# Two small tiles of a one-layer encoder kernel grow by 32 bytes

## The chip, the core and the metric

The kernel runs on one core of a Trainium2 chip. The core has TensorE for matmuls (its weight loads are shown as PEld), VectorE (DVE), ScalarE (ACT), GpSimd (POOL) and SyncE (SP), which issues most DMAs. The metric is the device time of one execution in microseconds. SBUF, the working memory, has 128 partitions; a tile takes the same address range in each of them, and "address" below means the byte offset within a partition.

## What is computed

One layer of a streaming encoder on 256 tokens of width 2048, in float32. RMS norm of x feeds one large projection; three mixers work on its columns (chunked attention, a diagonal state-space scan, an mLSTM matrix memory), are gated, merged and projected; then follow cross attention over 256 memory tokens and a SwiGLU block, each with a residual.

```python
h = _rms(x, norm_mix[i])
qa, ka, va, us, xm, vm, om, im, fm, gpre = jnp.split(h @ w_in[i], splits, axis=-1)
ya = _chunk_attention(qa, ka, va, ...)
ys = _s5(us, ...)
ym = _mlstm(xm, vm, om, im, fm, ...)
merged = (gates[:, :, 0] * (ya @ w_br_a[i]) + gates[:, :, 1] * (ys @ w_br_s[i])
          + gates[:, :, 2] * (ym @ w_br_m[i]))
x = x + merged @ w_out[i]
x = x + _mem_attention(_rms(x, norm_x[i]), mem_n, w_xq[i], w_xkv[i], g_xq[i], g_xk[i], w_xo[i])
x = x + _swiglu(_rms(x, norm_ffn[i]), w_gu[i], w_down[i])
```

## The kernel before

Every large product is done in three matmuls on the type float32r. Both operands are split into a high and a low part, and high x high, high x low and low x high are summed in PSUM. The weights come by DMA into `raw`, 2048 columns at a time; `split_w` (lines 110 to 118) makes `whi` on ScalarE (L116) and `wlo` on VectorE (L117). The activations are split once for each stage, by `split_act` (L206, L207, or L209, L210 with a gain), into the operand tiles `xT`, `mT`, `eT`, `x1T`, `oT`, `x2T`, `hT`, each with an `_h` and an `_l`.

Two helpers run the products. In `gemm_i` (L146, L147, L148) the activation tile is the loaded, stationary operand, 128 columns of it, and up to 512 columns of the split weights stream through. In `gemm_ii` (L169, L170, L171) the weights are loaded and 256 tokens of the activation stream. A matmul and the load of the next one's stationary operand overlap. Cross attention does its scores (L960) and its output (L986) in the same split type with 256 columns.

The stages run in this order: the input projection with the three mixers woven into it, the branch outputs, `w_out`, the memory's keys and values, the cross attention, `w_xo`, then gate and up projection (22 blocks) and the last projection `w_down`. The order on each engine is set when the program is built, by a scheduler that knows shapes and priorities.

Addresses come from pools. A pool gives each tag one or more buffers, and pools lie one behind the other in the order in which they are opened: `const`, `wp` (raw, whi, wlo), `scr` (small scratch tiles, among them `am`, 64 bytes in a partition, at L569), and behind `scr` all that the stages use: `poolA` (xT, later eT and oT), `p1`, `s5`, `p2`, `p3` (hT). Two pools are opened from the right end of the memory: `poolB` (L810; tags Bh and Bl for mT, x1T and x2T) and `px1` (the residual x1) to the left of it. A tile's size thus shifts all that is placed behind it. Sizes are rounded up to 32 bytes.

`am` holds 16 values for each partition, the mLSTM gate terms of 4 heads, 2 token tiles and 2 kinds. VectorE and ScalarE write it in `m_gates`; `m_core` reads columns of it as biases.

Of the kernel before, what the change touches and what calls it, by code (L numbers as in the profile page):

```python
# [9 lines left out]
F32 = mybir.dt.float32  # L10
F32R = mybir.dt.float32r
# [7 lines left out]
P = 128  # L19
T = 256  # L20
D = 2048
KD = D // P
# [30 lines left out]
def tile_block(ctx: ExitStack, tc: tile.TileContext, a: dict, out: bass.AP):  # L53
# [6 lines left out]
    scr = ctx.enter_context(tc.tile_pool(name="scr", bufs=4))  # L60
# [3 lines left out]
    def nm(s):  # L64
        uid[0] += 1
        return f"{s}_{uid[0]}"
# [5 lines left out]
    def sm():  # L72
        t = ps.tile([P, 512], F32, tag="sm", name=nm("sm"))
        return t
# [184 lines left out]
    def vexp(dst, src, n):  # L259
        def tt(s):  # L260
            return p1.tile([P, 32], F32, tag="ve_" + s, name=nm("ve_" + s), bufs=1)[:, :n]
        x, kf, r, pz = tt("x"), tt("k"), tt("r"), tt("p")
        V.tensor_scalar(x, src, -120.0, 120.0, ALU.max, ALU.min)
        V.tensor_scalar(kf, x, 1.4426950408889634, MAGIC, ALU.mult, ALU.add)
        V.tensor_scalar(kf, kf, MAGIC, None, ALU.subtract)
        V.scalar_tensor_tensor(r, kf, -0.693359375, x, ALU.mult, ALU.add)
        V.scalar_tensor_tensor(r, kf, 2.12194440e-4, r, ALU.mult, ALU.add)
        c = [1.0 / 5040, 1.0 / 720, 1.0 / 120, 1.0 / 24, 1.0 / 6, 0.5, 1.0]
        V.tensor_scalar(pz, r, c[0], None, ALU.mult)
        for ci in c[1:]:  # L270
            V.scalar_tensor_tensor(pz, pz, ci, r, ALU.add, ALU.mult)

        k1 = tt("k1")
        V.tensor_scalar(k1, kf, 0.5, MAGIC, ALU.mult, ALU.add)
        V.tensor_scalar(k1, k1, MAGIC, None, ALU.subtract)
        V.tensor_tensor(kf, kf, k1, ALU.subtract)
        V.tensor_scalar(pz, pz, 1.0, None, ALU.add)
        for kx in (k1, kf):
            ki = p1.tile([P, 32], I32, tag="ve_i", name=nm("ve_i"), bufs=2)[:, :n]
            V.tensor_scalar(kx, kx, 127.0, 8388608.0, ALU.add, ALU.mult)  # L280
            V.tensor_copy(ki, kx)
            V.tensor_tensor(pz, pz, ki.bitcast(F32), ALU.mult)
        V.tensor_copy(dst, pz)
# [247 lines left out]
    def m_gates():  # L531

        g = ymv["if"]
        zf = g[:, :, 4:8]

        def t8(s):
            return scr.tile([P, 2, 4], F32, tag="g8_" + s, name=nm("g8_" + s), bufs=1)
        fl = lambda x: x.rearrange("p t h -> p (t h)")
        az, e, y, y2, s_ = t8("az"), t8("e"), t8("y"), t8("y2"), t8("s")
        V.scalar_tensor_tensor(az, zf, -1.0, zf, ALU.mult, ALU.min)  # L540
        vexp(fl(e), fl(az), 8)
        V.tensor_scalar(y, e, 2.0, None, ALU.add)
        V.reciprocal(y, y)
        V.tensor_tensor(y, y, e, ALU.mult)
        V.tensor_tensor(y2, y, y, ALU.mult)
        V.tensor_scalar(s_, y2, 2.0 / 17, None, ALU.mult)
        for d in (15, 13, 11, 9, 7, 5, 3):
            V.scalar_tensor_tensor(s_, s_, 2.0 / d, y2, ALU.add, ALU.mult)
        V.scalar_tensor_tensor(s_, s_, 2.0, y, ALU.add, ALU.mult)
        V.tensor_scalar(az, zf, 0.0, None, ALU.min)  # L550
        V.tensor_tensor(az, az, s_, ALU.subtract)
        pt = sm()
        for t in range(2):
            PE.transpose(pt[0:4, t * P:(t + 1) * P], az[:, t], ident)
            PE.transpose(pt[0:4, T + t * P:T + (t + 1) * P], g[:, t, 0:4], ident)
        rows = p1.tile([4, 5, T], F32, tag="V", name="rows")
        V.tensor_copy(rows[:, 0:2], pt[0:4, :].rearrange("p (k t) -> p k t", k=2))
        on = cc[0:4, CC_ONE:CC_ONE + 1].to_broadcast([4, T])
        V.tensor_tensor_scan(rows[:, 2], on, rows[:, 0], 0.0, ALU.mult, ALU.add)
        V.tensor_tensor(rows[:, 0], rows[:, 1], rows[:, 2], ALU.subtract)  # L560
        V.tensor_tensor_scan(rows[:, 3], on, rows[:, 0], NEG, ALU.mult, ALU.max)
        V.tensor_tensor(rows[:, 1], rows[:, 2], rows[:, 3], ALU.add)
        V.tensor_scalar(rows[:, 4], rows[:, 3], -1.0, None, ALU.mult)
        pb = sm()
        for w in range(2):
            for t in range(2):
                c0 = (w * 2 + t) * 4
                PE.transpose(pb[:, c0:c0 + 4], rows[:, w, t * P:(t + 1) * P], ident[0:4, 0:4])
        am = scr.tile([P, 2, 2, 4], F32, tag="am", name="am", bufs=1)  # L569
        V.tensor_copy(am[:, 0], pb[:, 0:8].rearrange("p (t h) -> p t h", t=2))  # L570
        S.activation(am[:, 1], pb[:, 8:16].rearrange("p (t h) -> p t h", t=2), AF.Exp, scale=-1.0)
        ymv["rows"], ymv["am"] = rows, am
# [185 lines left out]
    for h in range(MH):  # L758
        off = gemm_i(xAh, xAl, KD, w_in, off, MD + (8 if h == 0 else 0), vm_evac(h))
        if h == 0:  # L760
            m_gates()
        m_core(h)
        run(bg_gen, 1)
# [44 lines left out]
    s5.release()  # L808

    poolB = tc.alloc_tile_pool(name="poolB", bufs=1, side="right")  # L810
    mTh = poolB.tile([P, KD, T], F32R, tag="Bh", name="mT_h")
    mTl = poolB.tile([P, KD, T], F32R, tag="Bl", name="mT_l")

    def to_operand(srcs, dh, dl, k0, gname=None):

# [102 lines left out]
        heads_T(kn, cons)  # L918

    fTh = poolB.tile([P, KD, T], F32R, tag="Bh", name="x1T_h")  # L920
    fTl = poolB.tile([P, KD, T], F32R, tag="Bl", name="x1T_l")
    for n in range(4):
        to_operand([x1[:, t, n * 512:(n + 1) * 512] for t in range(2)], fTh, fTl, 4 * n, "norm_x")
    finish_rstd(0, 2)
# [14 lines left out]
    for h in range(XH):  # L939
# [40 lines left out]
        for d2 in range(0, 4, 2):  # L980
# [8 lines left out]
            k = 4 * h + d2  # L989
            split_act(oTh[:, k:k + 2], oTl[:, k:k + 2], po.rearrange("p (k t) -> p k t", k=2))  # L990

    gTh = poolB.tile([P, KD, T], F32R, tag="Bh", name="x2T_h")
    gTl = poolB.tile([P, KD, T], F32R, tag="Bl", name="x2T_l")
    off = 0
    for n in range(4):
        off = gemm_i(oTh, oTl, KD, a["w_xo"], off, 512,
# [147 lines left out]
```

## Time and profile before

| what | value |
|---|---|
| median of 3 runs | 2039.26 us (2037.75 to 2039.5) |
| profiled execution, device time | 2038.49 us |
| its span, first to last instruction | 2036.7 us |
| mean granted TensorE clock | 1.000 |
| HBM traffic | 374.06 MB read, 2.10 MB written, 185 GB/s over the span |

Times in the profile are microseconds, and durations of single instructions are nanoseconds. A row of a group reads: line, engine, operation, output <- inputs, shape, count, then busy time, mean duration of one, and the idle time of the engine before it with what ended that idle time. In the timeline a row has the start, the duration, the instruction and how many were merged. Durations of matmuls are modelled and overlap; their starts are what can be subtracted. In the table of stretches, busy time and number of instructions stand for PE, PEld, DVE, ACT and POOL in this order, then the granted clock, the DMA share and GB/s.

### The profile page before, as it was taken

What the parts mean: (1) busy time and instruction counts of PE and PEld (TensorE: products, weight loads), DVE (VectorE), ACT (ScalarE), POOL (GpSimd) and SP (SyncE); (2) the same over time, 40 slices, a digit from 0 to 9 for tenths busy, and PEclk for the clock granted to TensorE, in tenths of its full rate; (3) what the DMA queues carried; (4) which work ended last, traced back from release to release, by engine and by line L of the source; (5) the groups of instructions that cost most, each with busy time, mean ns of one, the idle gap of its engine ahead of it and who ended that gap; (6) DMA issues with size and microseconds to landing.
All of it is one profiled execution on the core that took longest, in us unless ns stands there. A gap on an engine that the chain in (4) does not pass through costs nothing.

```text
span 2036.7 us, 25145 instructions
## 1 busy us (share of the span) xinstructions
PE 2025.7 (99%) x9880; PEld 1666.2 (82%) x9880; DVE 1251.8 (61%) x1804; ACT 975.1 (48%) x1332; POOL 78.6 (4%) x142
## 2 busy tenths in 40 slices
PE   9999999999999999999999999999999999999999
PEld 7998888787777788888888888888888888888887
DVE  8967796769897857644545655454544444444443
ACT  7555655555444444554545545444444444433332
POOL 1001202000000000011000100000000000000000
PEclk9999999999999999999999999999999999999999
DMA  8554455555555656755454435555555555555553
GB/s 310 185 175 170 143 177 186 168 183 178 180 191 179 203 182 221 258 202 186 166 186 166 153 138 184 186 186 184 173 185 185 186 184 186 186 186 196 197 199 132
DMA packets 60406, 377.78 MB, mean 185 GB/s; under 512 B 6912, under 2 KB 8064, under 8 KB 18816
## 3 DMA queue, kind: packets, MB, share of 16 engines
q1 hardware_dynamic: 56880, 367.42, 51.5%
q0 software_dynamic: 2112, 6.82, 1.3%
q10 hardware_dynamic: 1296, 1.95, 0.3%
q8 instruction: 77, 1.26, 0.3%
q14 instruction: 41, 0.34, 0.0%
HBM read 374.06 MB, written 2.10 MB: 185 GB/s over the span
## 4 chain that ended last, share of the span: by engine, by line
PE 96%; DVE 1%; POOL 1%; DMA 1%; ACT 1%; issue 0%; SPq 0%; DVEq 0%; POOLq 0%; ACTq 0%
PE acc L146 28%; PE acc L148 28%; PE acc L147 28%; PE acc L170 2%; PE acc L169 2%; PE acc L171 2%; PE sm L820 1%; PE sm L411 1%; DMA raw<-in_w_in_dram 1%; PE sm L960 1%; PE sm L986 1%; DVE wlo L117 1%; PE sm L904 0%; PE sm L215 0%; PE sm L456 0%
## 5 line engine op out<-in xcount | busy, mean ns | idle before, releaser
L117 DVE TENSOR_TENSOR wlo<-raw,whi 128x1024 fp32r<-128x1024 f32 (+2 forms) x700 | 834.6, 1194 | 685.7 <-ACT whi L116 683.0
L116 ACT CAST whi<-raw 128x1024 fp32r<-128x1024 f32 (+2 forms) x700 | 715.1, 1025 | 911.6 <-PE acc L148 742.2
L146 PE MATMUL acc<-whi,x2T_h 128*128 128x512 f32 x704 | 281.2, 399 | 0.0
L148 PE MATMUL acc<-whi,x2T_l 128*128 128x512 f32 x704 | 277.9, 395 | 0.0
L147 PE MATMUL acc<-wlo,x2T_h 128*128 128x512 f32 x704 | 277.2, 394 | 0.0
L147 PE MATMUL acc<-wlo,xT_h 128*128 128x512 f32 (+2 forms) x704 | 264.8, 377 | 1.5 <-DVE wlo L117 1.4
L148 PE MATMUL acc<-whi,xT_l 128*128 128x512 f32 (+2 forms) x704 | 263.9, 376 | 0.0
L146 PE MATMUL acc<-whi,xT_h 128*128 128x512 f32 (+2 forms) x704 | 262.5, 377 | 0.3 <-ACT whi L116 0.3
L148 PEld LDWEIGHTS acc<-whi,x2T_l 128*128 128x128 f32 x704 | 132.2, 188 | 33.5
L147 PEld LDWEIGHTS acc<-wlo,x2T_h 128*128 128x128 f32 x704 | 132.2, 188 | 31.3
L146 PEld LDWEIGHTS acc<-whi,x2T_h 128*128 128x128 f32 x704 | 132.2, 188 | 30.2
L147 PEld LDWEIGHTS acc<-wlo,xT_h 128*128 128x128 f32 x704 | 132.0, 188 | 29.6 <-DVE wlo L117 3.2
L146 PEld LDWEIGHTS acc<-whi,xT_h 128*128 128x128 f32 x704 | 131.5, 188 | 28.3 <-issue 1.3
L148 PEld LDWEIGHTS acc<-whi,xT_l 128*128 128x128 f32 x704 | 132.1, 188 | 26.8 <-issue 0.7
L146 PE MATMUL acc<-whi,hT_h 128*128 128x512 f32 x352 | 139.1, 395 | 0.0
L147 PE MATMUL acc<-wlo,hT_h 128*128 128x512 f32 x352 | 139.1, 395 | 0.0
L148 PE MATMUL acc<-whi,hT_l 128*128 128x512 f32 x352 | 139.0, 395 | 0.0
L169 PE MATMUL acc<-xT_h,whi 128*128 128x256 f32 x352 | 99.7, 283 | 2.1 <-DVE ev L625 2.1
L148 PE MATMUL acc<-whi,eT_l 128*128 128x512 f32 x256 | 101.6, 397 | 0.0
L147 PE MATMUL acc<-wlo,eT_h 128*128 128x512 f32 x256 | 101.4, 396 | 0.0
L146 PE MATMUL acc<-whi,eT_h 128*128 128x512 f32 x256 | 101.2, 395 | 0.0
L170 PE MATMUL acc<-xT_l,whi 128*128 128x256 f32 x352 | 100.2, 285 | 0.0
(376 smaller groups left out, 2832.2 us busy)
## 6 DMA issues: line engine op xcount, KB each, us to landing
raw<-in_w_gu_dram SPq DMA_DIRECT2D x88, 1024.0 KB, 4.7
raw<-in_w_in_dram SPq DMA_DIRECT2D x68, 1024.0 KB, 4.9
raw<-in_w_down_dram SPq DMA_DIRECT2D x44, 1024.0 KB, 4.7
raw<-in_w_xkv_dram SPq DMA_DIRECT2D x32, 1024.0 KB, 4.8
raw<-in_w_ii_dram SPq DMA_DIRECT2D x22, 1024.0 KB, 4.9
raw<-in_w_out_dram SPq DMA_DIRECT2D x16, 1024.0 KB, 4.8
raw<-in_w_xq_dram SPq DMA_DIRECT2D x16, 1024.0 KB, 4.8
raw<-in_w_xo_dram SPq DMA_DIRECT2D x16, 1024.0 KB, 4.8
```

The lines of the kernel that those rows point to most:

```text
L116: S.copy(hi[:, :n], raw[:, c0:c1])
L117: V.tensor_tensor(lo[:, :n], raw[:, c0:c1], hi[:, :n].bitcast(F32), ALU.subtract)
L146: PE.matmul(o, sh, h, start=(kt == 0), stop=False)
L147: PE.matmul(o, sh, lw, start=False, stop=False)
L148: PE.matmul(o, xl[:, kt, t * P:(t + 1) * P], h, start=False, stop=(kt == nk - 1))
L169: PE.matmul(po, h, xh[:, kt, :], start=(kt == 0), stop=False)
L170: PE.matmul(po, h, xl[:, kt, :], start=False, stop=False)
L171: PE.matmul(po, lo[:, j * P:(j + 1) * P], xh[:, kt, :], start=False, stop=(kt == nk - 1))
L411: PE.matmul(pb[e][:, i * T:(i + 1) * T], bT[q:q + 32, i, c, :], u[q:q + 32, c, :], start=True, stop=True, tile_position=(q, 0))
L820: PE.transpose(px[:, j * T + t * P:j * T + (t + 1) * P], srcs[t][:, (kp + j) * P:(kp + j + 1) * P], ident)
L960: PE.matmul(pS[:, t * T:(t + 1) * T], qx[:, qi, d, t * P:(t + 1) * P], kx[:, ki, d], start=(d + i == 0), stop=(d == 3 and i == 2))
L986: PE.matmul(po[:, j * T:(j + 1) * T], vx[:, vi, m, c0:c0 + P], pT[pi][:, m * T:(m + 1) * T], start=(m + i == 0), stop=(m == 1 and i == 2))
```

## The change

`am` is allocated with 24 columns where 16 are used (96 bytes for 64), and viewed in its old shape. The tag Bl of `poolB` gets 8 columns more (32 bytes), for its three tiles, through a helper that returns the old view. Nothing else differs.

```diff
-        am = scr.tile([P, 2, 2, 4], F32, tag="am", name="am", bufs=1)
+
+        am = scr.tile([P, 24], F32, tag="am", name="am", bufs=1)[:, 0:16]
+        am = am.rearrange("p (w t h) -> p w t h", w=2, t=2)
         V.tensor_copy(am[:, 0], pb[:, 0:8].rearrange("p (t h) -> p t h", t=2))
...
     poolB = tc.alloc_tile_pool(name="poolB", bufs=1, side="right")
+
+    def operand_low(name):
+
+        t = poolB.tile([P, KD * T + 8], F32R, tag="Bl", name=name)
+        return t[:, 0:KD * T].rearrange("p (k t) -> p k t", t=T)
     mTh = poolB.tile([P, KD, T], F32R, tag="Bh", name="mT_h")
-    mTl = poolB.tile([P, KD, T], F32R, tag="Bl", name="mT_l")
+    mTl = operand_low("mT_l")
...
-    fTl = poolB.tile([P, KD, T], F32R, tag="Bl", name="x1T_l")
+    fTl = operand_low("x1T_l")
...
-    gTl = poolB.tile([P, KD, T], F32R, tag="Bl", name="x2T_l")
+    gTl = operand_low("x2T_l")
```

What that does to the addresses, from the built programs (bytes within a partition; in brackets the remainder by 64):

| tile | before | after |
|---|---|---|
| whi, first buffer | 36672 (0) | 36672 (0) |
| wlo, first buffer | 53056 (0) | 53056 (0) |
| t2k, first buffer | 74560 (0) | 74560 (0) |
| am | 83040 (32) | 83040 (32) |
| gt, first buffer | 84384 (32) | 84416 (0) |
| xT_h, eT_h, oT_h, hT_h | 88864 (32) | 88896 (0) |
| xT_l, eT_l, oT_l | 105248 (32) | 105280 (0) |
| hT_l | 133920 (32) | 133952 (0) |
| qx, kx, vx | 154400, 162592, 170784 (32) | 154432, 162624, 170816 (0) |
| x1 | 180192 (32) | 180160 (0) |
| mT_h, x1T_h, x2T_h | 196576 (32) | 196544 (0) |
| mT_l, x1T_l, x2T_l | 212960 (32) | 212928 (0) |

The steps within these tiles are multiples of 512 bytes, so each operand of a matmul has the remainder of its tile. On each engine the instructions, their order and their waits are the same in both programs.

## The prediction

> **What bounds the kernel now.** I read the page first: the busy times, the clock row, and the chain of work that ended last.
>
> ```profile
> span 2036.7 us, 25145 instructions
> PE 2025.7 (99%) x9880; PEld 1666.2 (82%) x9880; DVE 1251.8 (61%) x1804; ACT 975.1 (48%) x1332; POOL 78.6 (4%) x142
> PEclk9999999999999999999999999999999999999999
> PE 96%; DVE 1%; POOL 1%; DMA 1%; ACT 1%; issue 0%; SPq 0%; DVEq 0%; POOLq 0%; ACTq 0%
> ```
>
> TensorE is busy for 99% of the span, its granted clock is never held back, and 96% of the chain that sets the end is matmuls. So the time is the number of matmuls times the distance from the start of one to the start of the next, which I call the pitch. The change touches no instruction: engine by engine, the built program has the same instructions in the same order with the same waits as before, and only addresses differ. It can act only through the pitch, or through a slower or faster vector, scalar or DMA access, and those are off the chain.
>
> The duration of one matmul in the profile is not its pitch (0.39 us against 0.23 us below), since matmuls overlap in the array. The pitch comes from the timeline of TensorE alone: first start, last start, and the number of matmuls in the stretch. This is the last projection, with 512 moving columns in each matmul, and under it the row of the busy times by stretch that gives the count (x195).
>
> ```profile
> 1814.73 0.39 PE L147 MATMUL acc<-wlo,hT_h 128*128 128x512 f32 x1
> ...
> 1859.99 0.39 PE L146 MATMUL acc<-whi,hT_h 128*128 128x512 f32 x1
> 1815.00:1860.00 45.00, 45.00 (x195) 36.13 (x194) 20.94 (x19) 16.80 (x17) 0.00 (x0) 1.00 0.56 199
> ```
>
> From 1814.73 to 1859.99 there are 194 steps, so the pitch is 45.26 / 194 = 233.3 ns. There is no gap in it: the stretch is 100% busy, with VectorE and ScalarE below half. The program has 7,344 such matmuls of 512 columns (60 blocks of 96 in the projections with 16 row tiles, 8 x 48 and 4 x 36 in the branch outputs, 4 x 264 in the last projection), 7344 x 0.2333 = 1713 us, 84% of the span. About 1,830 more of split type have 256 or 264 columns.
>
> **What lies where.** Of each operand I use the start address within 64 bytes, from the built program. Before the change the split weights whi and wlo and the buffers t2k start on a multiple of 64; every activation operand (xT, eT, oT, hT, mT, x1T, x2T, and yg, kx, qx, vx, ya, ym) starts 32 bytes past one. After the change all of these start on a multiple. In gemm_i (the 512-column matmuls) the weights stream and the activations are the ones that are loaded, so there only the **loaded** operand is off the 64 bytes now. In gemm_ii it is the other way round: the **streamed** operand is off.
>
> **The change part by part.** First the load of the stationary operand, from the groups by line and form: two of split type (hT_l of gemm_i is off by 32, whi of gemm_ii lies on 64) and two of transposes, which load their source (ev lies on 64, gt is off).
>
> ```profile
> L148 PEld LDWEIGHTS acc<-whi,hT_l 128*128 128x128 f32 x352 | 66.0, 187 | 16.1
> L169 PEld LDWEIGHTS acc<-xT_h,whi 128*128 128x128 f32 x352 | 66.3, 188 | 2.4 <-DVE ev L625 2.3
> L904 PEld LDWEIGHTS sm<-cc,ev 128*128 128x128 f32 x64 | 7.7, 141 | 1.2
> L820 PEld LDWEIGHTS sm<-cc,gt 128*128 128x128 f32 x88 | 10.9, 140 | 2.4
> ```
>
> 187 ns off the boundary against 188 on it, 140 against 141: the recorded load does not know where its operand lies. Nor is it what the pitch waits for: the load of the next matmul takes 187 of the 233 ns, beside the matmul. For the 7,344 wide matmuls I therefore take **0 us**: their streamed operand is on the boundary already, and moving the loaded one changes nothing that these rows show. That leaves one thing unexplained, the level of 233.3 ns itself, and the rivals price it.
>
> Second, the narrow matmuls, where both cases of the streamed operand occur. The timeline of four stretches with 256 columns and full pipelines follows, with the counts of the first two: gemm_ii on xT, gemm_ii on yg (both stream off, load on), the scores of the cross attention (kx and qx, both off), its output (t2k streams on, vx loads off). A merged row holds n matmuls and runs to the end of the last one.
>
> ```profile
> 93.88 0.28 PE L170 MATMUL acc<-xT_l,whi 128*128 128x256 f32 x1
> ...
> 104.30 0.28 PE L171 MATMUL acc<-xT_h,wlo 128*128 128x256 f32 x1
> 94.10:104.30 10.20, 10.20 (x89) 10.20 (x88) 8.06 (x17) 5.45 (x9) 0.00 (x0) 1.00 0.55 169
> 747.30 0.28 PE L171 MATMUL acc<-yg,wlo 128*128 128x256 f32 x1
> ...
> 759.32 0.28 PE L169 MATMUL acc<-yg,whi 128*128 128x256 f32 x1
> 747.50:759.40 11.90, 11.90 (x104) 11.90 (x103) 7.82 (x12) 8.58 (x16) 0.00 (x0) 1.00 0.60 196
> 1111.11 2.31 PE L960 MATMUL sm<-kx,qx 128*128 128x256 f32 x18
> 1128.65 2.61 PE L986 MATMUL sm<-t2k,vx 128*128 128x256 f32 x21
> ```
>
> The pitches are 10.42 / 88 = 118.4 ns for xT, 12.02 / 103 = 116.7 for yg, (2.31 - 0.28) / 17 = 119.4 for kx with qx, and (2.61 - 0.28) / 20 = 116.5 for t2k with vx. Two facts point against a large effect. yg streams off the boundary and is as fast as t2k, which streams on it. And gemm_ii, whose loaded operand has always been on the boundary, has the level per column of the wide matmuls (116.7 / 256 = 0.456 ns, 233.3 / 512 = 0.456 ns). So I cost the third kind of edit, the streamed xT, at the way from 118.4 to 116.7: 1056 x 1.7 ns = -1.8 us. kx with qx goes from 119.4 to 116.5: 96 x 2.9 ns = -0.3 us. For the remaining narrow ones (mLSTM values, queries and keys, and the two groups above that are at 116.5 and 116.7) I take 0.
>
> Third, VectorE and ScalarE read and write the moved tiles. Each pair of rows below has the same work, on the boundary first and off it second.
>
> ```profile
> L116 ACT CAST whi<-raw 128x1024 fp32r<-128x1024 f32 x658 | 688.1, 1049 | 880.5 <-PE acc L148 731.2 <-DMA raw<-in_w_in_dram 66.1 <-PE acc L170 15.0
> L206 ACT CAST kx<-kTm 128x1024 fp32r<-128x1024 f32 x4 | 4.2, 1052 | 6.1 <-PE sm L960 6.1
> L117 DVE TENSOR_TENSOR wlo<-raw,whi 128x1024 fp32r<-128x1024 f32 x658 | 804.0, 1224 | 663.1 <-ACT whi L116 661.0
> L207 DVE TENSOR_TENSOR kx<-kTm,kx 128x1024 fp32r<-128x1024 f32 x4 | 4.9, 1224 | 0.5 <-ACT kx L206 0.5
> ```
>
> 1049 against 1052 and 1224 against 1224 ns: nothing, and what there is lies under the matmuls. If that cover were gone, the 3 ns of ScalarE on each of its 1,332 instructions would be 4 us at most. The weight DMAs land in raw, which does not move.
>
> **Sum.** The profiled execution took 2038.49 us (span 2036.7 and 1.8 around it): 2038.49 - 1.8 - 0.3 = 2036.4. The median of the three runs is 0.8 above that execution, so the forecast is **2037.2 us**, 0.1% under the median, which a measurement of this kernel cannot tell from no change (it tells about 0.2%, 4 us).
>
> [...]
>
> **Rivals.** *Faster: a 64-byte piece costs a slot.* If operands are fetched in pieces of 64 bytes, a load of 512 bytes that starts 32 past a boundary touches nine pieces and not eight. For it speaks the order of the narrow pitches: both off 119.4, one off 116.5 to 118.4. Against it speak the equal load rows. The smallest price is what an aligned loaded operand is worth from kx with qx to xT: 1.0 ns per load, 7344 x 1.0 = 7 us; if it goes with the columns, 15 us; the narrow ones go on from xT by the 2.9 ns of an aligned stream, 1836 x 2.9 = 5 us. That is -12 to -20 us, 2018 to 2027, and I name 2022. The other end is that the whole excess goes. Its bound comes from the plain f32 transposes:
>
> ```profile
> 991.28 1.80 PE L820 MATMUL sm<-cc,x 128*128 128x128 f32 x15
> ```
>
> (1.80 - 0.27) / 14 = 109.3 ns for 128 columns, 0.854 ns a column, 1.87 times the 0.456 of the split type (0.27 is the duration of one). Were the split type exactly twice as fast, an estimate from these rows, 512 columns would take 218.6 ns: 7344 x 14.7 = 108 us, and 1836 x 9.1 = 17 us on the narrow ones, down to 1914 us. [...]
>
> *Slower: equal places collide.* kx with qx is also the only pair above whose two operands start at the same place within 512 bytes (288), and it is the slowest. After the change whi and wlo (320) meet the loaded xT, eT, oT, hT and ya at 320 too, 4,128 of the wide matmuls; mT, x1T and x2T lie at 448, ym and ys at 256. If equal places make the two reads meet in the same part of the memory, each pays 2.9 ns per 256 columns: 4128 x 5.8 = 24 us, and gemm_ii about 1 us: 2063. If equality within 64 bytes is enough, all 7,344 pay, 43 us, with the narrow ones 2083. It decides from the point where a pair in step is slower than a pair 32 bytes out of step; the trace has that one pair for it, and no pair that is both on 64 against it.
>
> **How the numbers follow.** No effect (2034 to 2041): 0.42. Faster: 0.37, of which 0.20 between 2008 and 2033 and 0.17 below. Slower: 0.21, about half at 24 us and half at 44 us. The range 1980 to 2066 leaves out about 0.09 below (most of the excess gone) and 0.10 above (all pairs collide); it is wide because the bounds of the one unknown, the wide pitch with both operands on 64, are 218.6 and 239.1 ns.
>
> **What would show it.** After the change the same stretch of the last projection has to read 233.3 ns a matmul by first start, last start and count; gemm_ii on xT has to fall to 116.7 and L960 to 116.5. A wide pitch of 231 to 232 means the piece rule, 219 to 222 that alignment was the whole excess; 239 with hT at 320, and 233 with x2T at 448, means collision within 512 bytes. If PEld durations or the granted clock change, the reason is one that I have not priced. The forecast is wrong if the wide pitch moves by 0.6 ns or more.

## The result and the profile after

The changed kernel takes 2014.7 us (median of 4 runs, 2013.28 to 2018.08) against 2039.08 for the kernel before on the same chip. The ratio is 0.9884 with a 95% interval of 0.9867 to 0.9901: 1.2% or about 24 us faster. The forecast of 2037.2 us, no effect, was wrong; the measured time lies inside its range. One of the four executions of the kernel with all operands 32 bytes past (further down) took 3643.47 us at a granted clock of 0.771, and the ratio given there uses the other three.

The page after, in the lines that answer to those shown of before: span, busy times, granted clock, and the chain by engine.

```profile
span 2011.5 us, 25145 instructions
PE 2000.9 (99%) x9880; PEld 1670.1 (83%) x9880; DVE 1249.9 (62%) x1804; ACT 975.0 (48%) x1332; POOL 78.6 (4%) x142
PEclk9999999999999999999999999999999999999999
PE 93%; DVE 4%; DMA 2%; ACT 0%; issue 0%; POOL 0%; SPq 0%; DVEq 0%; ACTq 0%
```

TensorE is busy for 99% of the span, as before, and lost 24.8 us of busy time, while the span fell by 25.2. VectorE and ScalarE are where they were. So the gain is in the pitch of the matmuls, and the timeline of TensorE after the change shows in which. First the last projection (hT), then gate and up (x2T), and under it the same stretch of x2T in the kernel before; each time the first and the last of a stretch without gaps, and the row of the busy times by stretch with the count.

```profile
1777.59 0.39 PE L148 MATMUL acc<-whi,hT_l 128*128 128x512 f32 x1
...
1815.90 0.39 PE L146 MATMUL acc<-whi,hT_h 128*128 128x512 f32 x1
1777.90:1816.10 38.20, 38.20 (x170) 31.65 (x169) 17.27 (x15) 14.77 (x14) 0.00 (x0) 1.00 0.55 196
...
1273.21 0.40 PE L147 MATMUL acc<-wlo,x2T_h 128*128 128x512 f32 x1
...
1313.58 0.39 PE L146 MATMUL acc<-whi,x2T_h 128*128 128x512 f32 x1
1273.50:1313.80 40.30, 40.30 (x174) 32.42 (x173) 19.15 (x18) 17.86 (x18) 0.00 (x0) 1.00 0.53 185
```

x2T before:

```profile
1291.12 0.39 PE L147 MATMUL acc<-wlo,x2T_h 128*128 128x512 f32 x1
...
1331.49 0.39 PE L146 MATMUL acc<-whi,x2T_h 128*128 128x512 f32 x1
1291.40:1331.70 40.30, 40.30 (x174) 32.43 (x173) 19.16 (x18) 17.82 (x18) 0.00 (x0) 1.00 0.53 184
```

hT: 38.31 / 169 = 226.7 ns, where it was 233.3. x2T: 40.37 / 173 = 233.4 ns, and before the same 40.37 / 173 = 233.4. Both groups had their loaded operand moved onto a multiple of 64, and only one of them became faster. The reader should stop here: whatever the reason is, "on a multiple of 64" by itself is not it.

The narrow matmuls answer in the other direction. These are gemm_ii on xT, and the output of the cross attention, now at L993.

```profile
61.83 0.28 PE L169 MATMUL acc<-xT_h,whi 128*128 128x256 f32 x1
...
81.99 0.28 PE L169 MATMUL acc<-xT_h,whi 128*128 128x256 f32 x1
62.00:82.00 20.00, 20.00 (x169) 20.00 (x169) 18.51 (x61) 9.54 (x10) 0.00 (x0) 1.00 0.54 195
1112.89 2.80 PE L993 MATMUL sm<-t2k,vx 128*128 128x256 f32 x22
```

gemm_ii: 20.16 / 168 = 120.0 ns, 118.4 before. L993: (2.80 - 0.28) / 21 = 120.0, 116.5 before. Both became slower.

The account by groups, from the mean step between neighbouring starts in each group (steps with a wait in them left out), before and after:

| group | matmuls | ns before | ns after | us |
|---|---|---|---|---|
| xT, eT, oT, ya streamed against, 512 columns | 3072 | 233.3 | 227.2 | -18.6 |
| hT, 512 | 1056 | 233.3 | 226.7 | -7.0 |
| ym, ys, 512 | 336 | 233.4 | 229.2 | -1.4 |
| mT, x1T, x2T, 512 | 2880 | 233.4 | 233.0 | -1.0 |
| gemm_ii on xT, 256 | 1056 | 118.3 | 119.8 | +1.6 |
| mLSTM values, 256 | 288 | 117.3 | 119.8 | +0.7 |
| yg, xs, kx, t2k streamed, 256 | 396 | 117.7 | 118.1 | +0.2 |

The sum is -25.5 us, and the span fell by 25.2. Nothing is left to explain outside the pitch. The last row is a mixture: the matmuls on xs went from 118.0 to 116.2 ns, yg from 116.7 to 117.8, t2k with vx from 116.8 to 119.4. kx with qx stayed, 119.3 before and 119.0 after: both came onto a multiple of 64, and the distance between them stayed the same.

### The profile page after: what moved, and what is told of

It reads as the page before. It is cut to its first block, busy times and chain, and to the rows that moved or that the text cites. A ratio compares the mean times of both kernels' runs of the same rounds, so it can differ in the third digit from the quotient of the medians.

```text
span 2011.5 us, 25145 instructions
## 1 busy us (share of the span) xinstructions
PE 2000.9 (99%) x9880; PEld 1670.1 (83%) x9880; DVE 1249.9 (62%) x1804; ACT 975.0 (48%) x1332; POOL 78.6 (4%) x142
## 4 chain that ended last, share of the span: by engine, by line
PE 93%; DVE 4%; DMA 2%; ACT 0%; issue 0%; POOL 0%; SPq 0%; DVEq 0%; ACTq 0%
PE acc L147 27%; PE acc L146 27%; PE acc L148 27%; PE acc L170 2%; PE acc L169 2%; PE acc L171 2%; DVE wlo L117 2%; DMA raw<-in_w_in_dram 2%; PE sm L827 1%; PE sm L993 1%; PE sm L967 1%; PE sm L411 1%; ACT whi L116 0%; DVE s2k L442 0%; PE sm L911 0%
## 5 line engine op out<-in xcount | busy, mean ns | idle before, releaser
L146 PE MATMUL acc<-whi,x2T_h 128*128 128x512 f32 x704 | 279.0, 396 | 0.0
L147 PE MATMUL acc<-wlo,x2T_h 128*128 128x512 f32 x704 | 278.9, 396 | 0.0
L148 PE MATMUL acc<-whi,x2T_l 128*128 128x512 f32 x704 | 278.0, 395 | 0.0
L147 PE MATMUL acc<-wlo,xT_h 128*128 128x512 f32 (+2 forms) x704 | 262.3, 373 | 1.8 <-DVE wlo L117 1.6
L148 PE MATMUL acc<-whi,xT_l 128*128 128x512 f32 (+2 forms) x704 | 261.1, 372 | 0.0
L146 PE MATMUL acc<-whi,xT_h 128*128 128x512 f32 (+2 forms) x704 | 259.7, 373 | 0.3 <-ACT whi L116 0.3
L148 PEld LDWEIGHTS acc<-whi,x2T_l 128*128 128x128 f32 x704 | 132.2, 188 | 31.7
L146 PEld LDWEIGHTS acc<-whi,x2T_h 128*128 128x128 f32 x704 | 132.2, 188 | 31.5
L147 PEld LDWEIGHTS acc<-wlo,x2T_h 128*128 128x128 f32 x704 | 132.2, 188 | 31.5
L147 PEld LDWEIGHTS acc<-wlo,xT_h 128*128 128x128 f32 x704 | 132.4, 188 | 27.3 <-DVE wlo L117 4.4
L146 PEld LDWEIGHTS acc<-whi,xT_h 128*128 128x128 f32 x704 | 131.8, 188 | 24.8 <-issue 1.3
L148 PEld LDWEIGHTS acc<-whi,xT_l 128*128 128x128 f32 x704 | 132.4, 188 | 23.3 <-issue 0.7
L147 PE MATMUL acc<-wlo,hT_h 128*128 128x512 f32 x352 | 137.0, 389 | 0.0
L146 PE MATMUL acc<-whi,hT_h 128*128 128x512 f32 x352 | 137.0, 389 | 0.0
L148 PE MATMUL acc<-whi,hT_l 128*128 128x512 f32 x352 | 136.9, 389 | 0.0
L148 PE MATMUL acc<-whi,eT_l 128*128 128x512 f32 x256 | 100.2, 391 | 0.0
L147 PE MATMUL acc<-wlo,eT_h 128*128 128x512 f32 x256 | 99.9, 390 | 0.0
L146 PE MATMUL acc<-whi,eT_h 128*128 128x512 f32 x256 | 99.8, 390 | 0.0
```

The source lines that it names most:

```text
L146: PE.matmul(o, sh, h, start=(kt == 0), stop=False)
L147: PE.matmul(o, sh, lw, start=False, stop=False)
L148: PE.matmul(o, xl[:, kt, t * P:(t + 1) * P], h, start=False, stop=(kt == nk - 1))
```

## The experiments

**Theories.** R: what counts is the distance between the start of the streamed and the start of the loaded operand, within some period; xT, eT, oT and hT came to the same place within 512 bytes as the weights (320), and mT, x1T and x2T did not (448). B: each operand's own boundary of 64. A: the loaded operand's own place, whatever the weights do. All kernels below have the same instructions in the same order as the changed one; only paddings differ. Diffs are against the changed kernel.

**The two halves apart.** First the change on `am` without that on poolB:

```diff
-        t = poolB.tile([P, KD * T + 8], F32R, tag="Bl", name=name)
+        t = poolB.tile([P, KD * T + 0], F32R, tag="Bl", name=name)
```

> Only the am half of the change; the three poolB tiles stay 480 bytes past a multiple of 512 as before. Theory R (what counts is the distance between the starts of the streamed and the loaded operand within 512 bytes): the wide pitch of hT stays at 226.7 ns and that of x2T at 233.3, so the whole gain is here: 2014 to 2016 us. Rival B (what counts is that each operand starts on a multiple of 64): the poolB tiles lose what their half of the change gave them; the trace after the change shows nothing of a gain there, so if B holds in any form the time is between 2014 and 2020 us.

Measured 2016.01 us, ratio 0.9887 (0.9872 to 0.9902): all of the gain within the interval is in the 32 bytes on `am`. hT is at 226.7 ns, x2T at 233.3.

Then the poolB half alone:

```diff
-        am = scr.tile([P, 24], F32, tag="am", name="am", bufs=1)[:, 0:16]
+        am = scr.tile([P, 16], F32, tag="am", name="am", bufs=1)[:, 0:16]
```

> Only the poolB half of the change; all that lies left stays 32 bytes past a multiple of 64. Theory R: the distance of the poolB tiles goes from 160 to 128 bytes, both at 233.3 ns in the traces, so no change: 2038 to 2040 us. Rival B: mT, x1T and x2T with their weights both on 64 give up to 6.7 ns for each of 2,880 wide matmuls: 2020 us.

Measured 2036.31 us, ratio 0.9983 (0.9974 to 0.9993), 3.4 us faster than before; B's 2020 did not come. The x2T stretch:

```profile
1290.44 0.39 PE L147 MATMUL acc<-wlo,x2T_h 128*128 128x512 f32 x1
...
1330.87 0.39 PE L147 MATMUL acc<-wlo,x2T_h 128*128 128x512 f32 x1
1290.70:1330.90 40.20, 40.20 (x175) 32.59 (x174) 19.19 (x18) 17.90 (x18) 0.00 (x0) 1.00 0.52 185
```

40.43 / 174 = 232.4 ns, so 1.0 ns on 2,880 matmuls, 2.9 us, makes this small gain. R had expected none. At this distance the same group ran at 233.4 in the changed kernel and at 232.4 here: the same distance can give either, and no run shows why.

**Boundary or distance.** All operands of the wide matmuls and the weights start 32 bytes past a multiple of 64, at equal places (352 within 512 bytes; only ym and ys lie elsewhere, at 288); the weights are shifted by a longer `mhalf` in front of them:

```diff
-    mhalf = const.tile([P, 4], F32, name="mhalf")
+    mhalf = const.tile([P, 12], F32, name="mhalf")[:, 0:4]
...
-        t = poolB.tile([P, KD * T + 8], F32R, tag="Bl", name=name)
+        t = poolB.tile([P, KD * T + 32], F32R, tag="Bl", name=name)
```

> All operands of the wide matmuls, the split weights too, start 32 bytes past a multiple of 64, and at the same place within 512 bytes (352); ya too, but ym and ys at 288. Theory R: equal places, so 226.7 ns for xT, eT, oT, hT and for mT, x1T and x2T too, 2,880 x 6.7 = 19 us below the changed kernel: 1994 to 1997 us. Rival B: every operand is off 64, so at least the 233.3 ns of before everywhere, 2039 us or more. Rival A (the loaded operand's own place within 512 bytes counts, 320 being a good one): 352 is another place for it, so the gain of 24 us is lost or partly lost, 2020 to 2045 us.

Measured 1998.43 us, ratio 0.9796 (0.9777 to 0.9816). Its x2T stretch:

```profile
1271.58 0.39 PE L147 MATMUL acc<-wlo,x2T_h 128*128 128x512 f32 x1
...
1310.79 0.39 PE L146 MATMUL acc<-whi,x2T_h 128*128 128x512 f32 x1
1271.90:1311.00 39.10, 39.10 (x174) 32.38 (x173) 19.15 (x18) 17.91 (x18) 0.00 (x0) 1.00 0.55 190
```

39.21 / 173 = 226.6 ns, with no operand on a multiple of 64. B has fallen. The time is 1.4 us over what R had. A expected at least part of the gain to go, and it did not: 352 for the loaded operand goes with 226.7 here, and 320 goes with 226.7 in the changed kernel, each with weights at the same place. That alone would leave both places good ones; the first kernel of the map below settles it, where xT lies at 352 and the weights at 320, and the pitch is 233.2.

**The rest of the gain.** The poolB tiles at the place of the weights, by 40 columns of padding and not 8:

```diff
-        t = poolB.tile([P, KD * T + 8], F32R, tag="Bl", name=name)
+        t = poolB.tile([P, KD * T + 40], F32R, tag="Bl", name=name)
```

> The changed kernel with 128 bytes more on the low poolB tile, so that mT, x1T and x2T start 320 bytes past a multiple of 512 like the weights. Theory R: their pitch falls from 233.3 to 226.7 ns: 2014.7 - 19 = 1994 to 1997 us. Rival B: they were on a multiple of 64 already, so 2014 to 2016 us. Rival A: as R.

Measured 1997.82 us, ratio 0.9796 (0.9781 to 0.981); R had 1994 to 1997, just under it. The x2T stretch:

```profile
1272.37 0.39 PE L147 MATMUL acc<-wlo,x2T_h 128*128 128x512 f32 x1
...
1311.59 0.39 PE L146 MATMUL acc<-whi,x2T_h 128*128 128x512 f32 x1
1272.60:1311.80 39.20, 39.20 (x174) 32.47 (x173) 19.26 (x18) 17.91 (x18) 0.00 (x0) 1.00 0.55 189
```

39.22 / 173 = 226.7 ns. These tiles lay on a multiple of 64 before this step and lie on one after it; 128 bytes of distance were the difference.

**A map of places.** Four kernels, each executed once, have the operands at other places, by the padding of `am`, of the low poolB tile, and of a pad in front of hT. The first:

```diff
-        am = scr.tile([P, 24], F32, tag="am", name="am", bufs=1)[:, 0:16]
+        am = scr.tile([P, 32], F32, tag="am", name="am", bufs=1)[:, 0:16]
...
-        t = poolB.tile([P, KD * T + 8], F32R, tag="Bl", name=name)
+        t = poolB.tile([P, KD * T + 120], F32R, tag="Bl", name=name)
...
+    p3.tile([P, 8], F32, name="pad3")
     hTh = p3.tile([P, KF, T], F32R, name="hT_h")
```

> Loaded operands at other places within 512 bytes, weights at 320: xT, eT, oT and ya at 352, hT at 384, mT, x1T and x2T at 0. Theory R, strict form (only equal places give 226.7 ns, all else 229 to 233.4): all three groups at 229 to 233.4 ns, 7,008 wide matmuls lose up to 6.6 ns, about 2030 to 2042 us. Theory R, near form (what counts is how far one is from the other, little being good): 352 at 228 to 231, 384 at 230 to 233, 0 at 233. Narrow gemm_ii on xT leaves equality and goes from 119.8 to 116.7 ns, -3 us in either form.

Measured 2026.58 us: xT, eT, oT and hT at 233.2 to 233.3 ns, x2T at 228.9. gemm_ii on xT fell to 116.8, as expected. The near form of R falls here: it had 228 to 231 ns for xT, 32 bytes away, and 233 for x2T. The strict form has the pitches, about, but its 2030 to 2042 us missed: x2T gained 4.5 ns a matmul.

The second and the third kernel differ from this one only in their numbers of padding.

> As the run before with xT, eT, oT and ya at 416, hT at 32, mT, x1T and x2T at 64, which is 256 bytes from the weights. Theory R with a period of 512 bytes: all at 229 to 233.4 ns, 2030 to 2042 us. Theory R with a period of 256 bytes: mT, x1T and x2T at 226.7 ns, 2,880 x 6.6 = 19 us less: 2011 to 2023 us.

Measured 2026.52 us. This is x2T, 256 bytes from the weights:

```profile
1292.83 0.39 PE L147 MATMUL acc<-wlo,x2T_h 128*128 128x512 f32 x1
...
1332.27 0.39 PE L147 MATMUL acc<-wlo,x2T_h 128*128 128x512 f32 x1
1293.10:1332.30 39.20, 39.20 (x175) 32.47 (x174) 19.20 (x18) 17.95 (x18) 0.00 (x0) 1.00 0.55 189
```

39.44 / 174 = 226.7 ns, the pitch of the kernel with all equal: at 256 bytes this group ran as at 0, which fits a period of 256 bytes and not one of 512. A second pair of places agrees: xT at 416 here and x2T at 160 in the next kernel, 256 bytes apart, are both at 234.2 ns. The time is over the 2011 to 2023 that was expected of this case, since xT, eT and oT sit at 234.2 to 234.3 ns here.

> xT, eT, oT and ya stay equal to the weights (320); hT at 128 (192 bytes away), mT, x1T and x2T at 160. Theory R, strict: hT and the poolB tiles at 229 to 233.4 ns, 3,936 x up to 6.6 = 26 us over the run with all equal (1997.8): 2010 to 2024 us. Near form: 233 for both, 2024 us.

Measured 2024.88 us: hT 233.3 ns, x2T 234.2, xT, eT and oT still at 227. The time is just over the 2024 of both forms. In the fourth kernel hT lies 16 bytes past equality (the low poolB tile has 72 columns of padding):

```diff
-    hTh = p3.tile([P, KF, T], F32R, name="hT_h")
-    hTl = p3.tile([P, KF, T], F32R, name="hT_l")
+    def past(name, c):
+        t = p3.tile([P, KF * T + c + 4], F32R, name=name)
+        return t[:, c:c + KF * T].rearrange("p (k t) -> p k t", t=T)
+    hTh, hTl = past("hT_h", 4), past("hT_l", 124)
```

> xT, eT, oT and ya equal to the weights; hT 16 bytes past equality (336), neither it nor its distance a multiple of 32; mT, x1T and x2T at 192. Theory R, strict: hT at 229 to 233.4 ns; near form: hT at 227 to 229. Rival B, in the weak form that a multiple of 64 is a condition beside equality: hT at 233.3 or more. mT, x1T and x2T at 229 to 233.4 in all. 2010 to 2024 us.

Measured 2022.78 us. The hT stretch:

```profile
1780.34 0.40 PE L148 MATMUL acc<-whi,hT_l 128*128 128x512 f32 x1
...
1819.78 0.39 PE L146 MATMUL acc<-whi,hT_h 128*128 128x512 f32 x1
1780.60:1820.00 39.40, 39.40 (x170) 31.92 (x169) 17.35 (x15) 14.71 (x14) 0.00 (x0) 1.00 0.54 191
```

39.44 / 169 = 233.4 ns. Being near did not help: hT, 16 bytes off equality, lost the whole 6.7 ns. The weak form of B would have this row too, but it fell with the kernel in which all lies 32 bytes past. hT starts on no multiple of 32 here, unlike all other places in the map, and no run has both operands 16 bytes past; that its start by itself costs the time is not excluded.

Put together, by the distance from the start of the loaded to the start of the streamed operand, modulo 256 bytes. Each figure is the mean step of a group in one of the kernels; where several kernels have the distance, the lowest and the highest of them:

| distance | ns, 512 columns | ns, 256 columns |
|---|---|---|
| 0 | 226.7 to 227.9 | 119.0 to 119.8 |
| 32 | 233.3 | 116.7 to 117.3 |
| 64 | 228.9 to 229.3 | 117.8 |
| 96 | 233.3 to 233.5 | 119.9 |
| 128 | 232.4 to 233.3 | 119.9 |
| 160 | 234.1 to 234.3 | 117.7 to 118.8 |
| 192 | 233.3 | 116.2 |
| 224 | 233.1 to 233.3 | 118.2 to 118.8 |
| 240 | 233.3 | - |

**One of three.** With all equal, hT_l alone is put 32 bytes away (this kernel and the next hold the 40 columns of padding, and their diffs are against the kernel with all equal):

```diff
     hTh = p3.tile([P, KF, T], F32R, name="hT_h")
+    p3.tile([P, 8], F32, name="pad3")
     hTl = p3.tile([P, KF, T], F32R, name="hT_l")
```

> The run with all equal, but hT_l alone 32 bytes further (352); hT_h stays equal to the weights. In the last projection the order is L146 (hT_h, whi), L147 (hT_h, wlo), L148 (hT_l, whi), and while one streams, the operand of the next is loaded. Theory N (the stream meets the load of the next matmul): the step after the start of L147 is longer, the sum of three rises from 680.0 to about 686.7 ns, 352 x 6.7 = 2.3 us: 2000 us. Theory O (a matmul's own pair counts): the step after the start of L148 is longer, with the same sum. If the two operands only set a common rhythm, all three steps may be at 233.3, 7 us more: 2005 us.

Measured 2004.34 us. Seven matmuls in a row of the last projection, in the timeline; only the rows of L148 are shown, and between two of them lie one of L146 and one of L147:

```profile
1780.75 0.39 PE L148 MATMUL acc<-whi,hT_l 128*128 128x512 f32 x1
...
1781.45 0.39 PE L148 MATMUL acc<-whi,hT_l 128*128 128x512 f32 x1
...
1782.15 0.39 PE L148 MATMUL acc<-whi,hT_l 128*128 128x512 f32 x1
```

Two rounds of three take 1.40 us, 700 ns each: all of the gain is gone, 3 x 6.7 ns, though two of three loads are still in step. From all starts in the stage the three steps are 233.0 after L146, 239.0 after L147 and 228.0 after L148, so the longest is the one in which the odd operand is loaded, as N had it, but the sum is that of the third case, a common rhythm.

**The best version.** With ym and ys in place too:

```diff
+    p1.tile([P, 16], F32, name="padX")
     ymv["mw1"] = p1.tile([P, 16, T], F32, tag="X", name="mw1")
```

> The run with all equal, and ym and ys at 320 too (64 bytes more in front of their tile), so every wide matmul has equal places. 336 of them go from 229.2 to about 227.3 ns, -0.7 us against the run with all equal: about 1997 us, 0.979 of before. Theory R asks for 227 ns in all groups with 512 columns. yg moves to 128 bytes from its weights; 108 narrow matmuls, at most 0.3 us either way.

Measured 1997.47 us, ratio 0.9797 (0.9783 to 0.981), median of 5 runs. ym and ys are at 227.6 and 227.7 ns. It cannot be told from the version without this pad, but both are about 17 us faster than the changed kernel and 2.0% faster than the kernel before.

## Why the prediction was wrong, by its steps

- **What bounds the kernel** held: the change acts through the pitch and nowhere else, and the account by groups closes to 0.3 us.
- **The step that failed is the first of the sum**, "For the 7,344 wide matmuls I therefore take **0 us**: their streamed operand is on the boundary already, and moving the loaded one changes nothing that these rows show." The rows were the durations of the loads. They did not carry the pitch here: after the change they read the same, while the pitch of this very group fell by 6.6 ns.

```profile
L148 PEld LDWEIGHTS acc<-whi,hT_l 128*128 128x128 f32 x352 | 66.1, 188 | 13.6
```

  188 ns now and 187 before. What these 7,344 measured is -28.0 us. The prediction itself had named a move of 0.6 ns in this pitch as the sign of its being wrong. The time lay inside the range only because the range was wide enough to hold both rivals.
- **The argument from equal levels** (gemm_ii with its load on the boundary is as fast per column as gemm_i with its load off it) compared operands by their own boundary. By distance, yg and the wide matmuls of xT, eT, oT and hT all had their streamed operand 32 bytes past the loaded one, so the row could not tell them apart.
- **The narrow term had the wrong sign.** "the way from 118.4 to 116.7" became the way from 118.4 to 120.0: xT and its weights came to equal places, where the groups of 256 columns have mean steps of 119.0 to 119.8 ns, against 116.7 to 117.3 at 32 bytes. 1,056 of them cost 1.6 us and did not give 1.8. kx with qx, which was to reach 116.5, stayed at 119, since the two moved together.
- **The third term**, the vector and scalar work, was right: VectorE has 1,249.9 us of work against 1,251.8, ScalarE 975.0 against 975.1.
- **The faster rival** gave -12 to -20 us, near the measured -24, for a reason that the runs refute: with every operand 32 bytes past a multiple of 64, where this rival counts nine pieces and not eight, the wide pitch is 226.6 ns. That it came near is luck.
- **The colliding rival** named the quantity that the pitch followed in these runs, equal places of kx and qx, and was right for 256 columns: t2k with vx went from 116.5 to 120.0 when they became equal (other distances, 96 and 128 bytes, are as slow, 119.9). It carried the 2.9 ns over to 512 columns, where equal places ran fastest (hT at 226.7 ns, 233.3 before). Its sign was taken from the only pair in the trace, of another width; no row before had a wide matmul in step.

What is not settled: why the pitch follows the distance of the two operands, and why with a period of 256 bytes, which two pairs of places fit (226.7 ns at 0 and 256 bytes, 234.2 at 160 and 416); and why distance 0 is the fastest place tried at 512 columns (226.7 to 227.9 ns) and close to the slowest at 256 (119.0 to 119.8, where the highest is 119.9). With one operand of three out of step, the step of 239.0 ns is the one in which that operand is loaded. That the stream meets the load of the next matmul was the author's guess; no run here separates the two reads.

## What to carry to other kernels

Where float32r matmuls run back to back, measure the pitch by their starts, and look at the distance between the streamed and the loaded operand's addresses, modulo the 256 bytes that fitted here, before looking at each one's own boundary: for 512 columns distance 0 was worth 2.9% of the pitch (233.3 to 226.7 ns). A small scratch tile in front of the operands set that distance here for 4,128 wide matmuls at once (the 32 bytes on `am` alone took 2039.71 us to 2016.01), so a pad that makes all operands meet their weights is cheap to try, and it should be tried for each width apart. A row that is equal in two groups clears a suspect only if the groups differ in that suspect, and here neither group had its pair in step.

## What the runs showed of the hardware that was not expected

The wide pitch took few values, 226.7 and 233.3 ns above all, with 228.9 to 229.3 at a distance of 64 bytes, 232.4 at times at 128 and 234.1 to 234.3 at 160. Near equality was not enough: 16 bytes away, in the one kernel that has it, the pitch is 233.4. With one operand out of three out of step, all three steps moved (233.0, 239.0 and 228.0 ns, where the mean is 226.7 with all equal). No place tried here came under 226.6 ns for 512 columns with float32r.
